# A fourth room for raw weights in the pairs stage, and the attention's mask table kept in DRAM

## The chip, the cores and the metric

The kernel runs on one NeuronCore of a Trainium2 chip. The metric is the device time of one execution in microseconds (us), as the median of several runs. A core has a matrix engine (TensorE, PE in the profile; its weight loads are PEld), three engines for elementwise work (VectorE or DVE, ScalarE or ACT, GpSimd or POOL) and a queue engine (SyncE, SP). Each engine runs its own instructions strictly in the order that was fixed at compile time and waits on semaphores for the others. Transfers (DMAs) are issued from SP, ACT and POOL and run on 16 DMA engines that all of them share.

## What is computed

One layer of a hybrid encoder for 1024 tokens and 1024 channels: a pooling mixer and a stick-breaking attention side by side, merged by gates, then a squared-ReLU MLP.

```
h    = rmsnorm(x, g_pre_mix)
proj = h @ w_in                        # u_pool | q | k | v, 512 columns each
y_pool = multiscale_pool(u_pool) @ w_br_pool
# attention, 8 heads of 64, blocks of 128 queries, mask: s < t
z    = (q @ k.T) * 64 ** -0.5
log_1mb = where(mask, log_sigmoid(-z), 0)
tail = cumsum(log_1mb, reverse) - log_1mb
attn = where(mask, exp(log_sigmoid(z) + tail), 0)
y_sb = (attn @ v) @ w_br_sb
gates = sigmoid(h @ w_gate + b_gate)   # 2048 columns
m    = (gates[:, :1024] * y_pool + gates[:, 1024:] * y_sb) @ w_out
x    = x + rmsnorm(m, g_post_mix)
h2   = rmsnorm(x, g_pre_mlp)
x    = x + rmsnorm(square(relu(h2 @ w_up)) @ w_down, g_post_mlp)
```

## The kernel before

All products are made in three matmuls of 128 x 128 x 512 (`mm3`, lines 110 to 112): every float32 operand is split into a rounded high part and the rest as a low part, and high x high, high x low and low x high are summed in a PSUM bank. The split of a raw weight tile of 128 x 1024 is a cast on ScalarE (high part) and a subtraction on VectorE (low part): `split_weights` (lines 1193 and 1194), or `prep` (lines 76 and 78) for the ordinary products.

The stages follow each other: `phase_in` (load x, first projections, the mask table, the operands of the pairs), `phase_project` (the pairs stage), `phase_attention` (attention with the branch products between), `phase_post`, `phase_mlp`.

**The pairs stage.** The gates (16 column groups) and the queries and keys (4 groups each) are made two groups at a time by a scheme that saves one product in eight: 7 half products of 12 matmuls for a pair instead of 8. `PAIRS` lists the 12 pairs: five of gates, then q, k, q, k, then three of gates. A pair needs two raw weight tiles r1 and r2 of 512 KB. `sw_weights(i)` is a generator that loads both and makes from them four split weights, a step at a time: `a1` from r1; `a22` from half of r2, then an add in place (line 519); three more adds in place (lines 521 to 523); `sb` from the changed r1; `sa` from the changed r2. The splits `a1` and `sa` lie in a ring of three rooms (`whi`, `wlo`) of the pool `weights`. `a22` and `sb` have rooms of their own for even pairs (`a0`, `s0` in the pool `tops`) and for odd ones (`a1`, `s1` in the pool `sw`).

The raw tiles have three rooms: two with the tag `wraw` in the pool `weights` and one, `wrawx`, in the pool `sw`. `self.raws = itertools.cycle(range(3))` deals them out in turn: pair 1 has `wrawx` and a `wraw`, pair 2 a `wraw` and `wrawx`, pair 3 two `wraw`, and so on; pair 0, which is loaded before the pool `sw` exists, has two `wraw`.

In `phase_project` the loop over the pairs makes the products of pair i, and at each product it takes one step of `sw_weights(i + 1)`, whose first step issues the loads of pair i + 1 on SP. A load waits until the room's last reader is done. The products of pair i are, in this order: `a1` x b11 and `a1` x b21 (`begin`), `sb` x t2, `sa` x t3, `sa` x t1, `a22` x t4, `sb` x b22. The operands b11 to t4 were made in `phase_in`; t2, t3 and t4 lie in the pool `tops`. The results go from PSUM through VectorE (lines 684, 695 to 705) to `result`: gates through a sigmoid into DRAM (`gscr`), queries and keys split (lines 542 and 543) into two staging rooms and from there into DRAM (`qscr`). Beside the products runs `later`: the pooling mixer (lines 560 to 610, operand `pq` on line 595, stored to `yscr`) and, after it, the values' pairs (`vpair`, `vs`).

**What fixes the order.** The code is traced in program order, and a scheduler at compile time orders each engine's instructions by when its model takes them to be ready. `issue_after(ins)` keeps an instruction behind another one on the same queue. The engine then keeps to that order, whatever is late.

**Where tiles lie.** Pools are stacked in the scratchpad, and the tiles of a pool lie in the order of their first allocation, from its lowest address up. The pool `sw` is opened when the pool `in_a`, with the tiles of x, is closed, and takes its place; the pools of the attention (`gt`, `att` and others) take the place of `tops` and `sw`. Pools opened with `reuse_waits="tile"` wait tile by tile: a new tile's first write waits for the last reader of the old tiles on that place, and no other. Both pools share one end, which is where `tops` ends. In the pool `in_a` the tile of `xs[0][0]` and `xs[0][1]` lies lowest, then the one of `xs[0][2]` and `xs[0][3]` and so on; `x00` in the code is `xs[0][0:4]`. In `tops` t2, t4 and t3 are followed by `a0` and `s0`; the gates' four rooms `gt` and the two rooms `oT` of the pool `gt` cover `a0` and `s0`.

**The mask table.** `phase_in` makes on GpSimd a table of 128 x 1024 bytes (line 303, 0 or 1 for "not in the past") into `self.past`, which has a fixed place in the pool `const`. Its only reader is the scan of the attention, `tensor_tensor_scan` on VectorE (line 801), one for each head and block of 128 queries, 64 in all.

**The start of the attention.** At the end of `phase_project` SP loads the queries and keys of the first two heads (lines 771 and 772), the pooling mixer's result y (line 730), the first gates (line 891, `gt`) and the values (line 755, `v`). Then the branch products (`job_pool`) run between the first heads' scores: each has 12 matmuls into one of two PSUM banks `dbr`, which VectorE empties into the gate tile (line 907), and the score products go through a sigmoid on ScalarE (line 799) and the scan on VectorE.

Of the kernel before, what the change touches and what calls it, by code (L numbers as in the profile page):

```python
# [19 lines left out]
F32 = mybir.dt.float32  # L20
# [12 lines left out]
P = 128  # L33
# [7 lines left out]
O_QK = O_U + N_U  # L41
O_V = O_QK + N_QK
O_G = O_V + N_V
# [9 lines left out]
class Block:  # L53
# [113 lines left out]
    def build(self):  # L167
        tc, nc = self.tc, self.nc
# [11 lines left out]
        cp = tc.alloc_tile_pool(name="const", bufs=1, side="left")  # L180
        self.wp = tc.alloc_tile_pool(name="weights", bufs=1, side="left")
        self.big = tc.alloc_tile_pool(name="big", bufs=1, side="left")
        dp = tc.alloc_tile_pool(name="scratch", bufs=1, space=DRAM)
# [4 lines left out]
        self.tscr = [dp.tile([P, 4, H], F32, name=f"tscr{f}") for f in range(4)]  # L188
        self.wscr = [[dp.tile([P, 4, 512], F32, name=f"wscr{n}_{q}") for q in range(4)] for n in range(2)]
        self.wsums = self.weight_sums()  # L190
        self.uscr = [dp.tile([P, 1024], F32, name=f"uscr{i}") for i in range(4)]
        self.qscr = [[dp.tile([192 - 64 * i, 1024], F32, name=f"qscr{i}_{j}") for j in range(8)] for i in range(2)]
        self.vscr = dp.tile([1 + P * NK, H], F32, name="vscr")
# [12 lines left out]
        self.gn = cp.tile([P, 32], F32, name="gn")  # L206
        self.eye = cp.tile([P, P], F32, name="eye")

        self.past = cp.tile([P, 1024], mybir.dt.uint8, name="past")
        self.rcnt = cp.tile([P, 16], F32, name="rcnt")  # L210

        self.rp = tc.alloc_tile_pool(name="row", bufs=1, side="left")
# [22 lines left out]
    def phase_in(self):  # L235
        tc, nc = self.tc, self.nc
# [5 lines left out]
        pa = tc.alloc_tile_pool(name="in_a", bufs=1, side="right")  # L242
# [11 lines left out]
        for g in range(3):  # L254
            if g < 2:
                raw = self.wp.tile([P, 1024], F32, name="wraw", tag="wraw", bufs=2)
            else:
                raw = early["t2_hi"][:, 0:2, :].rearrange("p k n -> p (k n)")
# [38 lines left out]
        past = early["t2_hi"][:, 2:4, :].rearrange("p k n -> p (k n)")  # L297
# [2 lines left out]
            out=past, in_=past, pattern=[[1, 1024]], compare_op=ALU.is_ge, fill=0.0, base=P - 1024,  # L300
            channel_multiplier=-1,
        )
        nc.gpsimd.tensor_copy(self.past, past)

        zero = early["t2_lo"][:, 1, :].bitcast(BF16)[:, :H]
        nc.vector.memset(zero, 0.0)
# [7 lines left out]
        for h in range(2):  # L314
# [3 lines left out]
            for k in range(NK):  # L318
                g = self.gn[:, k : k + 1]
# [136 lines left out]
        banks = [self.dps.tile([P, H], F32, name="dv", tag="d") for _ in range(2)]  # L456
        banks += [self.zps.tile([P, H], F32, name="dv", tag=t, bufs=n) for t, n in (("at", 3), ("z", 2))]
        gen = v_steps(1, (1, 2, 3, 0), banks)
        self.raws = itertools.cycle(range(3))
        first = self.sw_weights(0)  # L460
        for m in range(4):
            next(gen)
# [4 lines left out]
            k = m  # L467
# [28 lines left out]

    PAIRS = [("g", i) for i in range(5)] + [("q", 0), ("k", 0), ("q", 1), ("k", 1)] + [("g", i) for i in range(5, 8)]

    def sw_weights(self, i):

        nc = self.nc
        kind, f = self.PAIRS[i]
        a, n = (O_G + f, 8) if kind == "g" else (O_QK + 2 * f + (kind == "k"), 4)
        raw = []
        for g in (a, a + n):
            if next(self.raws) < 2 or self.sw_pools[1] is None:
                t = self.wp.tile([P, 1024], F32, name="wraw", tag="wraw", bufs=2)
            else:
                t = self.sw_pools[1].tile([P, 1024], F32, name="wrawx", tag="wrawx")
            nc.sync.dma_start(t, self.w[g])  # L510
            raw.append(t)
        r1, r2 = raw
        a11, a12, a21, a22 = r1[:, :512], r1[:, 512:], r2[:, :512], r2[:, 512:]
        w = self.sw[i] = {}
        w["a1"] = self.split_weights(r1, self.wp, "w", 3)
        yield
        pool = self.sw_pools[i % 2]
        w["a22"] = self.split_weights(a22, pool, f"a{i % 2}", 1, 512)
        nc.vector.tensor_add(a22, a21, a22)
        yield  # L520
        nc.vector.tensor_add(a21, a11, a21)
        nc.vector.tensor_add(a11, a11, a22)
        nc.vector.tensor_add(a12, a12, a11)
        yield
        w["sb"] = self.split_weights(r1, pool, f"s{i % 2}", 1)
        yield
        w["sa"] = self.split_weights(r2, self.wp, "w", 3)
# [118 lines left out]
    def phase_project(self):  # L646
        tc, nc = self.tc, self.nc
        pw = tc.alloc_tile_pool(name="sw", bufs=1, side="right", reuse_waits="tile")
        self.sw_pools[1] = pw

        def part(name):
            return pw.tile([P, H], F32, name=name, tag=name, bufs=1 + (name == "u"))
# [35 lines left out]
        for i, (kind, f1) in enumerate(self.PAIRS):  # L688
            f2 = f1 + (8 if kind == "g" else 2)
            w = self.sw[i]  # L690
            nxt = self.sw_weights(i + 1) if i + 1 < len(self.PAIRS) else iter(())
            if i not in begun:
                begin(i)
            u, v, c22 = begun[i], part("v"), part("c22")
            nc.vector.tensor_add(u, u, product(w["sb"], 0, "t2"))
            nc.vector.tensor_add(v, u, product(w["sa"], 0, "t3"))
            d = product(w["sa"], 512, "t1")
            nc.vector.tensor_add(c22, v, d)
            nc.vector.tensor_add(u, u, d)
            self.result(kind, f2, 1, c22, -1.0)  # L700
            if i == len(self.PAIRS) - 2:
                begin(i + 1)
            nc.vector.tensor_add(v, v, product(w["a22"], 0, "t4"))
            self.result(kind, f2, 0, v, -1.0)
            nc.vector.tensor_add(u, u, product(w["sb"], 512, "b22"))
            self.result(kind, f1, 1, u, 1.0)
# [9 lines left out]
            tc.alloc_tile_pool(name=n, bufs=1, side="right", reuse_waits="tile")  # L716
            for n in ("gt", "att", "qk", "oo", "att_s")
        )
        jobs = [("p", e + d, h) for e in range(0, 8, 2) for h in range(2) for d in range(2)]
        jobs += [("m", e, 0) for e in range(8)]  # L720
        self.fetch_order, self.fetches = jobs, {}
# [937 lines left out]
```

## Time and profile before

| | |
|---|---|
| three runs | 1271.15, 1271.83, 1272.05 us; median 1271.83 |
| the profiled execution | 1273.34 us, its span 1271.3 us |
| granted TensorE clock, mean | 0.999 |
| PE busy | 1241.4 us, 98% of the span, 5707 matmuls |
| weight loads (PEld) | 1020.3 us, 80% |
| VectorE | 967.8 us, 76% |
| ScalarE | 631.0 us, 50% |
| GpSimd | 179.7 us, 14% |
| DMA | 283.00 MB, mean 223 GB/s |
| pairs stage, first to last matmul | 97.2 to 347.7 us |
| loads into `wraw` on line 510 | 16, of 512 KB |
| loads into `wrawx` on line 510 | 8, of 512 KB; 3.5 to 9.0 us from issue to landing, median 8.7 |

The span runs from the first to the last instruction; the profiled execution is a little longer than its span, and both are compared like with like. A row of a timeline gives the start (us from the span's start), the duration, the engine, the line of the kernel, the operation, the tile written and those read, and in brackets the idle time of the engine before it and what ended that. "SPq" is the queue of SyncE, where the duration is that of the issue and not of the transfer. A row of the waits gives who waited for whom, the total in us, the number of waits and the longest.

### The profile page before, as it was taken

To read this page: it belongs to the slowest core of one execution; us is meant where nothing else is said; L and a number is where in the kernel's file an instruction comes from. 1 tells how busy PE (TensorE), PEld (TensorE's weight loads), DVE (VectorE), ACT (ScalarE), POOL (GpSimd) and SP (SyncE) were. 2 spreads that over 40 slices of the span, in tenths; PEclk is the share of its full clock that TensorE was granted. 3 is DMA by queue.
4 is the path that set the end of the run, shared out by engine and by line. 5 is a ranking of instruction groups with operands and counts; after the bars stand their busy time and mean duration, and the time that the engine had idled before them with its cause. 6 is when DMAs were issued, how large, how long until landed. Compare 5 with 4: busy or idle time off the path is not lost.

```text
span 1271.3 us, 16191 instructions
## 1 busy us (share of the span) xinstructions
PE 1241.4 (98%) x5707; PEld 1020.3 (80%) x5707; DVE 967.8 (76%) x1311; ACT 631.0 (50%) x1010; POOL 179.7 (14%) x319
## 2 busy tenths in 40 slices
PE   9999999998999999999999999999999999999998
PEld 6887778877877888787778878888888888888887
DVE  8849687766578898877797879887865565776975
ACT  8147334333456666674556546455454443344452
POOL 1212112342101111101100002222121110001000
PEclk9999999999999999999999999999999999999999
DMA  6586878977899674457648677676559996556552
GB/s 218 172 226 165 249 189 252 314 240 247 294 359 345 203 213 118 117 129 219 215 135 263 198 248 257 226 241 221 180 182 335 306 300 229 197 198 248 191 198 67
DMA packets 110305, 283.00 MB, mean 223 GB/s; under 512 B 12464, under 2 KB 17584, under 8 KB 109072
## 3 DMA queue, kind: packets, MB, share of 16 engines
q1 hardware_dynamic: 65696, 165.28, 37.9%
q0 software_dynamic: 30992, 91.13, 25.1%
q10 hardware_dynamic: 13536, 25.57, 6.2%
q8 instruction: 45, 0.74, 0.2%
q14 instruction: 36, 0.29, 0.1%
HBM read 208.52 MB, written 94.37 MB: 238 GB/s over the span
## 4 chain that ended last, share of the span: by engine, by line
PE 69%; DVE 13%; DMA 10%; issue 5%; ACT 3%; POOL 0%; ACTq 0%; SPq 0%; DVEq 0%; POOLq 0%
PE d L110 15%; PE d L111 15%; PE d L112 15%; PE sw L110 3%; PE sw L111 3%; PE sw L112 3%; PE o L838 2%; DVE T L801 2%; PE dbr L111 2%; PE dbr L112 2%; PE dbr L108 2%; DVE wlo L78 1%; DMA yscr<-win 1%; DMA wraw<-w 1%; PE at L814 1%
## 5 line engine op out<-in xcount | busy, mean ns | idle before, releaser
L111 PE MATMUL d<-blo,whi 128*128 128x512 f32 (+1 forms) x456 | 172.3, 378 | 0.0
L112 PE MATMUL d<-bhi,wlo 128*128 128x512 f32 (+1 forms) x456 | 171.9, 378 | 0.0
L110 PE MATMUL d<-bhi,whi 128*128 128x512 f32 (+1 forms) x456 | 168.7, 378 | 0.0
L112 PEld LDWEIGHTS d<-bhi,wlo 128*128 128x128 f32 x456 | 85.8, 188 | 16.1
L111 PEld LDWEIGHTS d<-blo,whi 128*128 128x128 f32 x456 | 85.7, 188 | 15.8
L110 PEld LDWEIGHTS d<-bhi,whi 128*128 128x128 f32 x456 | 85.5, 188 | 16.0
L801 DVE TENSOR_TENSOR_SCAN T<-T,past 128x512 f32<-128x512 f32 (+3 forms) x64 | 84.8, 1345 | 8.7 <-ACT T L799 8.4
L111 PE MATMUL d<-b_lo,whi 128*128 128x512 f32 x196 | 76.2, 390 | 1.2 <-DVE b_lo L1085 1.2
L110 PE MATMUL d<-b_hi,whi 128*128 128x512 f32 x196 | 75.7, 390 | 0.1
L112 PE MATMUL d<-b_hi,wlo 128*128 128x512 f32 x196 | 74.2, 389 | 0.0
L78 DVE TENSOR_TENSOR wlo<-wraw,whi 128x1024 fp32r<-128x1024 f32 x45 | 54.9, 1220 | 15.2 <-ACT whi L76 13.5
L76 ACT CAST whi<-wraw 128x1024 fp32r<-128x1024 f32 x45 | 47.5, 1056 | 37.9 <-DMA wraw<-w 19.0
L1382 DVE TENSOR_TENSOR wlo<-slots_hi,whi 128x1024 fp32r<-128x1024 f32 x29 | 35.5, 1223 | 37.3 <-ACT whi L1380 37.3
L1380 ACT CAST whi<-slots_hi 128x1024 fp32r<-128x1024 f32 x29 | 30.5, 1051 | 67.2 <-PE d L111 61.0
L799 ACT ACTIVATE T<-z 128x256 f32<-128x256 f32 (+2 forms) x96 | 44.8, 492 | 38.1 <-PE z L797 34.9
L1380 ACT CAST whi<-slots_lo 128x1024 fp32r<-128x1024 f32 x27 | 28.4, 1054 | 60.6 <-PE d L111 50.3
L110 PE MATMUL sw<-h_hi,whi 128*128 128x512 f32 x144 | 56.5, 392 | 1.9 <-DVE c L684 1.3
L111 PE MATMUL sw<-h_lo,whi 128*128 128x512 f32 x144 | 56.1, 389 | 0.0
L112 PE MATMUL sw<-h_hi,wlo 128*128 128x512 f32 x144 | 55.5, 390 | 0.1
L824 ACT CAST ahi<-at 128x512 fp32r<-128x512 f32 (+1 forms) x96 | 44.1, 484 | 22.8 <-PE at L814 19.8
L825 DVE TENSOR_TENSOR alo<-at,ahi 128x512 fp32r<-128x512 f32 (+1 forms) x96 | 50.0, 542 | 6.7 <-ACT ahi L824 6.6
L1193 ACT CAST whi<-wraw 128x1024 fp32r<-128x1024 f32 (+1 forms) x29 | 26.7, 928 | 54.7 <-PE d L111 24.2
(447 smaller groups left out, 3451.6 us busy)
## 6 DMA issues: line engine op xcount, KB each, us to landing
wraw<-w SPq DMA_DIRECT2D x57, 512.0 KB, 5.0
ext_b<-ascr SPq DMA_DIRECT2D x40, 512.0 KB, 7.0
wscr<-w POOLq DMA_DIRECT2D x32, 512.0 KB, 9.6
slots_hi<-w SPq DMA_DIRECT2D x10, 1024.0 KB, 8.0
slots_lo<-w SPq DMA_DIRECT2D x10, 1024.0 KB, 8.6
qq<-qscr SPq DMA_DIRECT2D x32, 256.0 KB, 5.1
pscr<-p SPq DMA_DIRECT2D x32, 256.0 KB, 3.9
u<-pscr ACTq DMA_DIRECT2D x32, 256.0 KB, 4.3
```

Of the source, the lines that this page charges most:

```text
L76: nc.scalar.copy(hi, raw)
L78: self.lows.append(nc.vector.tensor_sub(lo, raw, hi.bitcast(F32)).ins)
L110: nc.tensor.matmul(ps, wh, rh, start=first and i == 0, stop=False)
L111: nc.tensor.matmul(ps, wh, rl, start=False, stop=False)
L112: self.last_mm = nc.tensor.matmul(ps, wl, rh, start=False, stop=last and i == n - 1).ins
L799: self.after = nc.scalar.activation(f, z[:, :n], AF.Sigmoid, scale=-1.0)
L801: nc.vector.tensor_tensor_scan(f[:, ::-1], f[:, ::-1], past[:, ::-1], 1.0, ALU.mult, ALU.max)
L824: self.att_hi = nc.scalar.copy(hi[:, c:], at[:, c:]).ins
L825: self.att_lo = nc.vector.tensor_sub(lo[:, c:], at[:, c:], hi[:, c:].bitcast(F32)).ins
L1193: self.last_hi = nc.scalar.copy(hi, src).ins
L1380: last_split[0] = nc.scalar.copy(hi, src).ins
L1382: last_split[1] = nc.vector.tensor_sub(lo, src, hi.bitcast(F32)).ins
```

## The change

The raw tiles get four rooms: even pairs have both in `wraw`, odd pairs both in `wrawx`, which now has two rooms. The loads move out of `sw_weights` into `sw_raw(i)`. Pair 0 is loaded where it was. Pair 1 is loaded as soon as the pool `sw` is open, so that the two `wrawx` rooms are the first and lowest tiles of that pool. Every later pair i + 2 is loaded at the head of the loop for pair i: its rooms are those of pair i, whose last step was taken during pair i - 1. Before, the loads of pair i + 1 were issued in pair i.

The second `wrawx` room takes 4 KB in each partition of a scratchpad that is full. The mask table's 1 KB in `const` is given up for it: the table is made in the pool `in_a`, stored to DRAM (`mscr`) from GpSimd's queue, and loaded again on SP when the attention's pools are opened, into the lowest place of the pool `gt` (the pool grows downwards by 1 KB, over the last KB of t3's low half; the rooms `gt` and `oT` keep their places). The load is queued behind the first head's keys.

```diff
+        self.mscr = dp.tile([P, 1024], mybir.dt.uint8, name="mscr")
...
-        self.past = cp.tile([P, 1024], mybir.dt.uint8, name="past")
...
-        nc.gpsimd.tensor_copy(self.past, past)
+        table = pa.tile([P, 1024], mybir.dt.uint8, name="table")
+        nc.gpsimd.tensor_copy(table, past)
+        nc.gpsimd.dma_start(self.mscr, table)
...
-        self.raws = itertools.cycle(range(3))
+        self.raw = {}
...
-    def sw_weights(self, i):
-
-        nc = self.nc
+    def sw_raw(self, i):
+
         kind, f = self.PAIRS[i]
         a, n = (O_G + f, 8) if kind == "g" else (O_QK + 2 * f + (kind == "k"), 4)
-        raw = []
+        self.raw[i] = []
         for g in (a, a + n):
-            if next(self.raws) < 2 or self.sw_pools[1] is None:
+            if i % 2 == 0:
                 t = self.wp.tile([P, 1024], F32, name="wraw", tag="wraw", bufs=2)
             else:
-                t = self.sw_pools[1].tile([P, 1024], F32, name="wrawx", tag="wrawx")
-            nc.sync.dma_start(t, self.w[g])
-            raw.append(t)
-        r1, r2 = raw
+                t = self.sw_pools[1].tile([P, 1024], F32, name="wrawx", tag="wrawx", bufs=2)
+            self.nc.sync.dma_start(t, self.w[g])
+            self.raw[i].append(t)
+
+    def sw_weights(self, i):
+
+        nc = self.nc
+        kind, f = self.PAIRS[i]
+        if i == 0:
+            self.sw_raw(0)
+        r1, r2 = self.raw[i]
...
         self.sw_pools[1] = pw
+        self.sw_raw(1)
...
             w = self.sw[i]
+            if i + 2 < len(self.PAIRS):
+                self.sw_raw(i + 2)
             nxt = self.sw_weights(i + 1) if i + 1 < len(self.PAIRS) else iter(())
...
+        self.past = self.gp.tile([P, 1024], mybir.dt.uint8, name="past")
+        with tc.issue_after(self.head_load):
+            nc.sync.dma_start(self.past, self.mscr)
```

More of the change, by code (lines that the diff above doesn't have):

```diff
@@ L497 @@
     PAIRS = [("g", i) for i in range(5)] + [("q", 0), ("k", 0), ("q", 1), ("k", 1)] + [("g", i) for i in range(5, 8)]
+    def sw_raw(self, i):
+        kind, f = self.PAIRS[i]
+        a, n = (O_G + f, 8) if kind == "g" else (O_QK + 2 * f + (kind == "k"), 4)
+        self.raw[i] = []
+        for g in (a, a + n):
+            if i % 2 == 0:
+                t = self.wp.tile([P, 1024], F32, name="wraw", tag="wraw", bufs=2)
+            else:
+                t = self.sw_pools[1].tile([P, 1024], F32, name="wrawx", tag="wrawx", bufs=2)
+            self.nc.sync.dma_start(t, self.w[g])
+            self.raw[i].append(t)
     def sw_weights(self, i):
@@ L502, in sw_weights @@
         kind, f = self.PAIRS[i]
-        a, n = (O_G + f, 8) if kind == "g" else (O_QK + 2 * f + (kind == "k"), 4)
-        raw = []
-        for g in (a, a + n):
-            if next(self.raws) < 2 or self.sw_pools[1] is None:
-                t = self.wp.tile([P, 1024], F32, name="wraw", tag="wraw", bufs=2)
-            else:
-                t = self.sw_pools[1].tile([P, 1024], F32, name="wrawx", tag="wrawx")
-            nc.sync.dma_start(t, self.w[g])
-            raw.append(t)
-        r1, r2 = raw
+        if i == 0:
+            self.sw_raw(0)
+        r1, r2 = self.raw[i]
         a11, a12, a21, a22 = r1[:, :512], r1[:, 512:], r2[:, :512], r2[:, 512:]
```

## The prediction

> **What bounds the kernel now.** I read the page first, then the busy time by stage, then what the matrix engine waited for in the stage that the change touches, and last the order of time around each of those waits.
>
> ```profile
> span 1271.3 us, 16191 instructions
> ...
> PE 1241.4 (98%) x5707; PEld 1020.3 (80%) x5707; DVE 967.8 (76%) x1311; ACT 631.0 (50%) x1010; POOL 179.7 (14%) x319
> ```
>
> The matrix engine (PE) is busy for 98% of the span, so an edit that adds or removes none of its matmuls can win only what PE stands idle, 1271.3 - 1241.4 = 29.9 us in all. The profiled execution took 1273.34 us, 2.0 us more than its span, and the median of the three runs is 1271.83, 1.5 us below it. I sum against the span and take the result off the median, because stalls are absolute times.
>
> ```profile
> 97.00:350.00 253.00, 242.76 (x1046) 195.64 (x1045) 189.44 (x276) 105.70 (x146) 60.66 (x96) 0.99 0.80 246
> 350.00:400.00 50.00, 46.78 (x256) 38.95 (x255) 40.44 (x65) 31.35 (x80) 4.96 (x17) 1.00 0.97 349
> ```
>
> The columns are the stretch, its length, the busy time (and instructions) of PE, its weight loads, VectorE (DVE), ScalarE (ACT) and GpSimd (POOL), the granted clock, the share of the DMA engines and their GB/s. The first row is the pairs stage, 97 to 350 us: PE is idle for 10.2 us of it. The second is the start of the attention, where the transfers fill 97% of the DMA engines. These two rows are the field: the change can win at most some 10 us in the first (a little more with the clock, below), and it puts one more transfer into the second. What PE waited for in the first:
>
> ```profile
> PE sw L110 <- DVE u L705: 3.3, 1, 3.3
> PE sw L110 <- ACT whi L1193: 2.6, 2, 1.5
> PE sw L110 <- DVE c L684: 1.3, 1, 1.3
> PE sw L110 <- DVE u L695: 0.8, 2, 0.4
> PE dm L111 <- DVE pq L595: 0.7, 1, 0.7
> PE sw L112 <- DVE wlo L1194: 0.7, 2, 0.5
> ```
>
> Columns: total us, times, longest. Only the second and the last row are waits for split weights (L1193, L1194). The others are waits for a PSUM bank that DVE had not yet emptied, or for the pooling's operand (L595).
>
> **Part 1: the fourth room and the early load.** Follow one late weight, the second raw tile of pair 2, through the queues.
>
> ```profile
> 127.86 1.22 DVE L1194 TENSOR_TENSOR s1lo<-wrawx,s1hi 128x1024 fp32r<-128x1024 f32 x1
> 129.12 0.33 SPq L510 DMA_DIRECT2D wrawx<-w  x1
> 137.26 1.23 DVE L581 TENSOR_TENSOR win<-u 128x1023 f32<-128x1023 f32 x1 [6.86 <-DMA yscr<-win]
> 138.06 0.62 ACT L1193 CAST a0hi<-wrawx 128x512 fp32r<-128x512 f32 x1 [9.32 <-DMA wrawx<-w]
> 145.85 0.39 PE L112 MATMUL sw<-ph,wm 128*128 128x512 f32 x1
> 146.65 1.04 ACT L1193 CAST whi<-wrawx 128x1024 fp32r<-128x1024 f32 x1 [0.48 <-DVE wrawx L521]
> 147.75 0.50 PE L110 MATMUL sw<-ht_hi,whi 128*128 128x512 f32 x1 [1.51 <-ACT whi L1193]
> ```
>
> The room comes free at 129.08, when the previous pair's last reader ends. The load goes out at 129.12 and lands 8.9 us later. DVE then stands idle for 6.86 us up to 137.26 (another transfer's doing), and after that it must do both the pooling and this tile's adds, so the split that PE needs comes at 146.65. With four rooms this tile goes into a room that pair 0 left long before; its adds fit into the idle 6.86 us, and the wait at 147.75 goes. PE lost 147.75 - 145.85 = 1.90 from start to start where 0.23 is usual, so 1.67, and some 0.1 more at the next matmul: about 1.2 times the wait shown. The next pair repeats it (the third row below is pair 0, at the very start):
>
> ```profile
> 161.81 0.62 ACT L1193 CAST a1hi<-wraw 128x512 fp32r<-128x512 f32 x1 [8.74 <-DMA wraw<-w]
> 171.62 0.50 PE L110 MATMUL sw<-ht_hi,whi 128*128 128x512 f32 x1 [1.08 <-ACT whi L1193]
> 104.23 0.50 PE L112 MATMUL sw<-ht_hi,wlo 128*128 128x512 f32 x1 [0.50 <-DVE wlo L1194]
> ```
>
> Direct gain: 2.6 us of L1193, and 0.2 of the 0.7 us of L1194, because the 0.5 us at 104.23 belong to pair 0, whose loads do not move: 2.8 x 1.2 = 3.4 us.
>
> Indirect gain: L684, L695 and L595 are late because DVE runs strictly in order and the same late adds (L519 to L523, 0.69 us each) stand ahead of them. Together 0.8 + 0.7 + 1.3 = 2.8 us, 3.4 with the factor. Its bounds are 0 (the adds only move, and other work stands there instead) and 3.4. I take the middle, 1.7, since DVE is busy for 75% of this stage and has the room, but waits for the pooling's and the values' transfers that the change leaves alone.
>
> The largest wait I leave in place:
>
> ```profile
> 298.70 0.39 PE L112 MATMUL sw<-h_hi,wlo 128*128 128x512 f32 x1
> 300.46 0.69 DVE L543 SCALAR_TENSOR_TENSOR ks<-v,ks 128x512 fp32r<-128x512 f32 x1 [3.87 <-ACT ks L542]
> 302.41 0.77 PE L110 MATMUL sw<-ht_hi,a1hi 128*128 128x512 f32 x1 [3.32 <-DVE u L705]
> 305.93 0.40 PE L112 MATMUL sw<-ht_hi,a1lo 128*128 128x512 f32 x1
> ```
>
> DVE stood 3.87 us for the staged keys, whose two rooms wait for their stores; no raw weight is in that chain. It costs 3.71 - 0.23 = 3.5 us, and then eight matmuls take 305.93 - 302.41 = 3.52 instead of 1.84, another 1.7: after the gap PE ran at half speed for a while. The Trainium skill, in "TensorE: Matmul & The Clock Gate" (HAM oscillation), says that an idle gap over about 3.4 us halves the clock; this gap of 3.71 us agrees. Gain 0; upper bound 5.2, if a new order of DVE takes L705 ahead of the keys.
>
> Pair 1 pays for the new layout. Both its raw tiles now lie lowest in the pool, over x tiles of the first phase, and the second covers the one holding x00[2] and x00[3], which the t2 fill still reads.
>
> ```profile
> 104.21 0.33 SPq L510 DMA_DIRECT2D wraw<-w  x1
> 110.11 0.69 DVE L1085 TENSOR_TENSOR ht_lo<-x,ht_hi 128x512 fp32r<-128x512 f32 x1
> 116.66 0.69 DVE L519 TENSOR_TENSOR wraw<-wraw 128x512 f32<-128x512 f32 x1
> 123.80 2.36 DVE L1194 TENSOR_TENSOR wlo<-wraw,whi 128x1024 fp32r<-128x1024 f32 x2
> ```
>
> So that load goes out at 110.8 instead of 104.2. Queued behind it on SP (in order) are only the later raw loads, which are early now. With the 8.9 us of above it lands at 119.7, 3.0 us after DVE wanted it at 116.66, and if all of that reached the split, done at 126.2, PE could lose up to 3 us. With a landing of under 5.8 us it is not late at all. What covers it is that PE is still on pair 0 and that DVE has the pooling's work to put ahead; I take 0 and keep the 3 for the range.
>
> **Part 2: the mask table through DRAM.** Its store at the start is one more issue on POOL (14% busy) behind a 1.4 us cast with nothing of the attention waiting: 0. The load is what counts. It needs 1 KB in each partition that lies over the end of t3's low half, so it waits for the last pair's t3 product; it is on SP, in order; and the first scan (L801) now waits for it.
>
> ```profile
> 339.30 0.39 PE L112 MATMUL sw<-ht_hi,wlo 128*128 128x512 f32 x1
> 344.17 0.47 SPq L730 DMA_DIRECT2D ylo<-yscr  x1
> 345.17 5.69 SPq L891 DMA_DIRECT2D gt<-gscr  x4
> 352.40 2.18 SPq L755 DMA_DIRECT2D v<-sscr  x4
> 353.50 0.69 DVE L907 TENSOR_TENSOR gt<-gt,dbr 128x512 f32<-128x512 f32 x1 [4.92 <-DMA gt<-gscr]
> 354.10 2.07 DVE L801 TENSOR_TENSOR_SCAN T<-T,past 128x512 f32<-128x512 f32 x2
> 354.24 0.50 PE L110 MATMUL dbr<-yhi,whi 128*128 128x512 f32 x1
> 356.08 0.66 DVE L907 TENSOR_TENSOR gt<-gt,dbr 128x512 f32<-128x512 f32 x1
> ```
>
> The gates' rooms (gt) lie over tiles that pair 10 was the last to read, so they are free before 339.5 and the order most likely is gates, table, values (v): the table goes out at about 352.4, in the place of the first value load. Its transfer, 128 KB in rows of 1 KB, is in no row of before. The nearest rows are these (size, median to landing):
>
> ```profile
> gt<-gscr SPq DMA_DIRECT2D x20, 256.0 KB, 5.1
> qscr<-qs POOLq DMA_DIRECT2D x16, 128.0 KB, 4.7
> v<-sscr SPq DMA_DIRECT2D x8, 512.0 KB, 6.9
> ```
>
> I take 4.0 us, a little under the row of its size (an estimate): landed at 356.4, so the scans move from 354.1 to 356.4, 2.3 us. Behind them on DVE is L907 at 356.08, which empties the bank of the second branch product and ends at 356.74, then 359.0. PE has two banks for these products. It began the third at 354.24, needs 12 x 0.23 = 2.7 us for it, and wants the second's bank at about 357.0, or 357.4 with the score matmuls between: 1.6 us lost. The later loads move back by 128 KB at 349 GB/s, 0.4 us. Cost 2.0 us. Lower bound: issued at 340 ahead of the gates, it lands by 347 even at the 6.9 us of the value loads, and costs only the 0.4. The upper bound is the third rival's. By the Trainium skill, "DMA: Bandwidth & Descriptors" (Anatomy of one DMA), a transfer costs some 2.0 us plus its bytes over 436 GB/s, an estimate of 2.3 us here, by which the scans would be 0.6 us late and the total some 1.6 us better; the 4.7 us of this trace's 128 KB row speak against it.
>
> The rest is free: the attention's first weight tiles find their rooms empty sooner (pair 11 no longer uses them), but PE waits for none of them there.
>
> **Sum.** -3.4 - 1.7 + 2.0 = -3.1 us: 1271.83 - 3.1 = 1268.7 us (a profiled execution of about 1270.2, span 1268.2). About 0.2%, 2.5 us, is what a measurement of this kernel can tell from no change.
>
> **Rivals.**
> - *More goes than I count.* With the adds early, DVE's order changes in the query and key pairs too, and the wait for L705 goes with the clock's 1.7 us: -3.1 - 5.2 = -8.3, 1263.5; with half of it, 1266.1. For it: DVE's adds stand in that queue too. Against: its chain is the staging rooms. Chance 0.17.
> - *The gain is eaten in the stage.* PE then waits for the next late thing: the pooling's transfers hold DVE for 6.86 us whatever the weights do. Only the direct 3.4 us go, new waits of 1 us come, and the table takes 2.0: -0.4, 1271.4. For it: L705 and L684 are late without weights. Chance 0.18.
> - *Slower: the table is late.* If it is queued among the value loads or lands like them (6.9 us in the median row), the scans start at 359.3 or later, 5 us behind, and PE, with two banks and in order, stands 4.5 us; a gap above the 3.7 us seen at 302.41 also brings the half clock, 1.7 us. Cost 6.2 + 0.4 against 5.1 won: +1.5, 1273.3; with the indirect gain absent, +3.2, 1275.0. It decides from a landing at about 358.5. For it: 97% DMA share there. Against: the table is small and was ready to go at 339.5. Chance 0.20.
> - That the change doesn't do what it says has little room: each load's room and place are in its lines.
>
> My forecast has the remaining 0.45, with its own range of 1266.7 to 1271.0.
>
> **The numbers.** Two thirds of the forecast's chance lies below -2.5 us (0.30), and all of the first rival: faster 0.47. Same: a third of the forecast (0.15), the second rival (0.18), and a quarter of the third (0.05): 0.38. Slower: the rest of the third, 0.15. The range 1264.5 to 1273.6 leaves out the first rival's better half and the third's worse half, some 0.2.
>
> **What would show it.** Right: no wait of ACT on wraw or wrawx over 2 us between pairs 2 and 5; the waits for whi L1193 gone; PE idle in the pairs stage about 5 us less; the first scan 1 to 3 us later behind its gate product, waiting for the table's load; L705's wait still there. Wrong: PE idle in the pairs stage unchanged though the loads are early (the second rival), or a gap of over 3.5 us at the first scans with a granted clock below 1 there (the third).

## The result and the profile after

Beside the kernel before on the same chip the changed kernel took 1262.09 us (four runs, 1259.63 to 1264.59) against 1271.94 us (four runs, 1271.15 to 1274.60): a ratio of 0.9925, 95% interval 0.9906 to 0.9943, or 9.9 us. The forecast was 3.1 us, and its range ended at 1264.5 us. The profiled execution took 1264.59 us, with a span of 1262.8 us, 8.5 us under that of before.

The page of the changed kernel, then its pairs stage and the start of the attention by stretch (columns as before):

```profile
span 1262.8 us, 16190 instructions
...
PE 1239.2 (98%) x5707; PEld 1021.2 (81%) x5707; DVE 968.6 (77%) x1311; ACT 630.7 (50%) x1010; POOL 180.4 (14%) x320
```

```profile
97.00:350.00 253.00, 248.51 (x1082) 202.80 (x1081) 193.67 (x282) 107.59 (x151) 60.68 (x96) 0.99 0.83 257
350.00:400.00 50.00, 47.67 (x264) 39.74 (x263) 42.91 (x73) 34.04 (x88) 6.91 (x24) 1.00 0.99 360
```

PE has 1082 matmuls in the first stretch where it had 1046, and is idle for 4.5 us there instead of 10.2. What it still waited for (the last row is already the attention):

```profile
PE sw L112 <- DVE wlo L1208: 2.7, 2, 2.2
PE sw L110 <- ACT vs L633: 0.9, 1, 0.9
PE z L808 <- ACT T L813: 0.8, 1, 0.8
```

The waits for `whi`, for `pq` and for every sum are gone, L705's among them. One wait is new, and large. To see where the time went I count the stage's `sw` products by pair: 84 matmuls for each pair (those of the pooling left out), the start of every 84th taken from the trace. Two stretches are enough. A is pairs 1 to 5, mostly gates, with all of the pooling's matmuls between them; B is pairs 6 to 11, most of the queries and keys and the last gates, to the last matmul of the stage. A pair that nothing holds up takes 19.0 us, and one with a group of the pooling beside it 20.4.

| | A, pairs 1 to 5 | B, pairs 6 to 11 |
|---|---|---|
| undisturbed | 4 x 20.4 + 19.0 = 100.6 us | 6 x 19.0 = 114.0 us |
| before | 225.5 - 117.9 = 107.6 us | 347.5 - 225.5 = 122.0 us |
| changed | 222.8 - 117.9 = 104.9 us | 338.4 - 222.8 = 115.6 us |

So A, where the forecast had put nearly all of its gain, gave 2.7 us, and B, where it had put some 0.8 us (its share of L684), 6.4 us. That makes 9.1 us of a span that is 8.5 us shorter; the rest of the span differs little. By pair: in A pairs 2 to 5 gained 6.6 us (86.8 to 80.2) and pair 1 lost 3.9; in B pair 8 gained 2.2 (the wait for L684), pair 9, with the wait for pair 8's sum L705 and the half clock behind it, 5.8, and pair 10 lost 1.4.

The new wait is in pair 1. PE first, then VectorE (DVE) ahead of it:

```profile
125.50 0.40 PE L111 MATMUL sw<-h_lo,whi 128*128 128x512 f32 x1
128.10 0.50 PE L112 MATMUL sw<-ht_hi,wlo 128*128 128x512 f32 x1 [2.20 <-DVE wlo L1208]
128.44 0.52 PE L110 MATMUL sw<-ht_hi,whi 128*128 128x512 f32 x1
128.76 0.63 PE L111 MATMUL sw<-ht_lo,whi 128*128 128x512 f32 x1
```

```profile
120.82 0.69 DVE L1208 TENSOR_TENSOR a0lo<-wraw,a0hi 128x512 fp32r<-128x512 f32 x1
...
123.22 0.69 DVE L527 TENSOR_TENSOR wraw<-wraw 128x512 f32<-128x512 f32 x1
...
125.62 0.69 DVE L529 TENSOR_TENSOR wraw<-wraw 128x512 f32<-128x512 f32 x1
126.22 0.69 DVE L693 TENSOR_TENSOR c<-u,sw 128x512 f32<-128x512 f32 x1
126.82 1.22 DVE L1208 TENSOR_TENSOR wlo<-wrawx,whi 128x1024 fp32r<-128x1024 f32 x1
```

The split that PE needs (pair 1's `sa`) ends at 128.04. Ahead of it stand three instructions on `wraw`, which is pair 2's: some 0.6 us each, 1.8 us. They can stand there because pair 2's weights are early now. Nor is there a hole in which they would be free, for DVE is busy in all of these 28 us (the fifth number):

```profile
104.00:132.00 28.00, 25.54 (x101) 19.77 (x102) 28.00 (x43) 19.05 (x27) 9.47 (x13) 0.94 0.83 209
```

Behind the wait the matmuls last 0.63 instead of 0.39 us, and the granted clock of the stretch is 0.94: PE runs at half speed for some 3 us. Pair 1 takes 24.6 us, 4.2 more than undisturbed and 3.9 more than in before.

The mask table did not go where I had put it:

```profile
334.94 0.56 SPq L732 DMA_DIRECT2D past<-mscr  x1
339.32 2.87 SPq L905 DMA_DIRECT2D gt<-gscr  x3
...
346.12 0.98 ACT L813 ACTIVATE T<-z 128x512 f32<-128x512 f32 x2 [3.75 <-DMA gscr<-c]
...
346.75 2.08 DVE L815 TENSOR_TENSOR_SCAN T<-T,past 128x512 f32<-128x512 f32 x2 [1.81 <-ACT T L813]
...
DMA to landing us min/median/max: 8.6/8.6/8.6
```

It is issued ahead of the gates (L905), lands 8.6 us later at 343.5, and the first scan waits for ScalarE's sigmoid (ACT, L813), which itself stood behind a gate's store. The table holds nothing up.

### The profile page after: what moved, and what is told of

Its sections match the earlier page's. It is cut to its first block, busy times and chain, and to the rows that moved or that the text cites. A ratio compares the mean times of both kernels' runs of the same rounds, so it can differ in the third digit from the quotient of the medians.

```text
span 1262.8 us, 16190 instructions
## 1 busy us (share of the span) xinstructions
PE 1239.2 (98%) x5707; PEld 1021.2 (81%) x5707; DVE 968.6 (77%) x1311; ACT 630.7 (50%) x1010; POOL 180.4 (14%) x320
## 4 chain that ended last, share of the span: by engine, by line
PE 73%; DMA 9%; DVE 8%; issue 6%; ACT 2%; POOL 1%; SPq 0%; ACTq 0%; DVEq 0%; POOLq 0%
PE d L112 17%; PE d L111 17%; PE d L110 17%; DMA vpair<-vscr 3%; PE o L852 2%; PE dbr L108 2%; PE dbr L111 2%; PE dbr L112 2%; PE at L828 2%; DVE T L815 2%; DMA yscr<-win 1%; DMA qq<-qscr 1%; PE sw L112 1%; PE sw L111 1%; PE sw L110 1%
## 5 line engine op out<-in xcount | busy, mean ns | idle before, releaser
L813 ACT ACTIVATE T<-z 128x256 f32<-128x256 f32 (+2 forms) x96 | 45.2, 493 | 33.8 <-PE z L811 29.3
L838 ACT CAST ahi<-at 128x512 fp32r<-128x512 f32 (+1 forms) x96 | 44.1, 484 | 22.5 <-PE at L828 20.2
L1396 DVE TENSOR_TENSOR wlo<-slots_lo,whi 128x1024 fp32r<-128x1024 f32 x27 | 33.0, 1222 | 27.3 <-ACT whi L1394 27.0
```

Of the source, the lines that this page charges most:

```text
L813: self.after = nc.scalar.activation(f, z[:, :n], AF.Sigmoid, scale=-1.0)
L838: self.att_hi = nc.scalar.copy(hi[:, c:], at[:, c:]).ins
L1396: last_split[1] = nc.vector.tensor_sub(lo, src, hi.bitcast(F32)).ins
```

## The experiments

The theory after this profile: (1) in A the early weights remove the waits of pairs 2 and 3, but pair 2's adds, early too, push back pair 1's last split; (2) in B it isn't the lateness of the weights that went but an order on DVE. The scheduler made its order anew with the early weights in its model, and in pair 8 the sum that empties a PSUM bank now stands ahead of a split that waits for a staging room; (3) the table is free. The main rival to (2): the weights were late in B as well, and their adds held up the sums. In before, the order was ks<-v (L543, at 300.46), then an add, then L705. Now the sum is first:

```profile
290.04 0.68 DVE L716 TENSOR_TENSOR u<-u,sw 128x512 f32<-128x512 f32 x1
...
294.12 0.69 DVE L551 SCALAR_TENSOR_TENSOR ks<-v,ks 128x512 fp32r<-128x512 f32 x1 [1.30 <-ACT ks L550]
```

All twelve runs, in three groups; each group ran on one chip and has its own runs of the kernel before. A and B are of each one's profiled execution.

| kernel | median, us | before beside it, us | ratio (95%) | A, us | B, us |
|---|---|---|---|---|---|
| room_late | 1263.38 | 1269.96 | 0.9949 (0.9933 to 0.9966) | 106.6 | 115.1 |
| pair2_order | 1265.03 | 1269.96 | 0.9956 (0.9938 to 0.9973) | 105.3 | 119.0 |
| table_alone | 1268.84 | 1269.96 | 0.9990 (0.9978 to 1.0002) | 107.1 | 118.4 |
| late_all | 1264.99 | 1269.96 | 0.9969 (0.9956 to 0.9982) | 109.0 | 114.0 |
| before_order | 1269.21 | 1270.30 | 0.9987 (0.9972 to 1.0002) | 109.0 | 118.5 |
| order_back | 1265.39 | 1270.30 | 0.9964 (0.9949 to 0.9978) | 107.5 | 117.5 |
| late_gates | 1269.35 | 1270.30 | 0.9987 (0.9977 to 0.9998) | 112.4 | 114.0 |
| late_qk | 1265.20 | 1270.30 | 0.9954 (0.9938 to 0.9970) | 107.0 | 116.0 |
| changed_again | 1265.07 | 1269.99 | 0.9967 (0.9955 to 0.9979) | 106.5 | 115.8 |
| table_late | 1263.53 | 1269.99 | 0.9952 (0.9935 to 0.9968) | 107.7 | 115.0 |
| sums_first | 1258.65 | 1269.99 | 0.9913 (0.9899 to 0.9927) | 102.4 | 114.0 |
| before_sums | 1272.61 | 1269.99 | 1.0027 (1.0006 to 1.0048) | 111.0 | 117.4 |

**The changed kernel again.** 

> The changed kernel itself, unaltered, beside the other three. Theory: 6 to 10 us faster than the kernel before, as in its first two comparisons; in the profile the wait for wlo at 128 us, pair 2 to 8 without a wait over 1.5 us.

It came out 4.9 us faster by the medians, at the low end, with the wait at 128 us (2.38 us lost) and nothing over 1.5 us in pairs 2 to 8. Together with room_late (below), whose program has the same order on every engine, there are three measurements of the change: 9.9, 6.6 and 4.9 us. The sign is safe. The size varies with the chip and the executions, and the first one was the largest.

**room_late: does the earlier place in the code matter?**

```diff
-            if i + 2 < len(self.PAIRS):
-                self.sw_raw(i + 2)
...
-        if i == 0:
-            self.sw_raw(0)
+        if i != 1:
+            self.sw_raw(i)
```

> Four rooms, but the loads of pair i + 1 stand in the code where they stood before, at the first step of its weights, and not a pair sooner. Theory (the room does it: a load goes out when its room is free, wherever the code has it): the time of the changed kernel, 1262.1 us within 2.5, and all four raw loads of two pairs issued as in the changed kernel. Rival (the earlier place in the code does it): a part of the 9.8 us comes back, 1265 us or more.

1263.38 us, and in the pairs stage each engine's order of instructions is that of the changed kernel. SP issues nothing but these loads from the start of the stage until the first head's queries and keys at some 277 us, so a load goes out when its room is free. The room is the change; "a pair sooner" is only its name in the code.

**table_alone: the table without the room.** The table's part of the change's diff, put into the kernel before.

> The kernel before with the mask table through DRAM alone, three raw rooms as they were. Theory (the load is issued with the y loads, ahead of the gates, and is there before the first scan needs it): no difference, 1271.9 us within 1. Rival (my forecast's price, 2.0 us at the first scans, which the changed kernel hides behind some other gain): 1273.9 us.

1.1 us faster by the medians, an interval that holds no difference and leaves out the 2.0 us of cost. Its stage has before's order, and so it is a second profile of before's A and B: A 107.1, B 118.4 us. B is 3.6 us less than in the first profile, though the wait for the sum is there:

```profile
PE sw L110 <- ACT whi L1198: 2.6, 2, 1.5
PE sw L110 <- DVE u L707: 2.4, 1, 2.4
```

L707 is L705 of before. The 3.6 us lie in two places: pair 8 takes 19.0 us, without the wait for L684 (21.2 in before), and pair 9 takes 23.4 instead of 24.8. That B moves by this much between two executions of one order is the reason not to read the change's 6.4 us in B as its worth: against table_alone it is 2.5 to 3.4 us over the profiles with the changed order (115.0 to 115.8).

**table_late: nearer to the place that I had forecast.**

```diff
-        with tc.issue_after(self.head_load):
-            nc.sync.dma_start(self.past, self.mscr)
...
-                    self.load_values(0)
+                    with tc.issue_after(self.fetch_last):
+                        last = nc.sync.dma_start(self.past, self.mscr).ins
+                    with tc.issue_after(last):
+                        self.load_values(0)
```

> The changed kernel with the mask table's load queued behind the first gates and ahead of the values: the place that my forecast gave it. If the forecast's price for that place is right (landed at about 356 us, the first scans 2 us later, PE 1.6 + 0.4 us), it is 2 us slower than the changed kernel beside it. Rival (the first scan waits for ScalarE and the gates' adds anyway): within 0.7 us.

No slower than the changed kernel beside it (1263.53 against 1265.07 us).

```profile
342.65 0.38 SPq L749 DMA_DIRECT2D past<-mscr  x1
...
349.38 2.07 DVE L816 TENSOR_TENSOR_SCAN T<-T,past 128x512 f32<-128x512 f32 x2 [1.15 <-ACT T L814]
...
DMA to landing us min/median/max: 6.6/6.6/6.6
```

The table lands at 349.3 us, 0.1 us before the scan starts, and what the scan waits for last is still ScalarE. So the load is free here too, but with nothing to spare. It stands behind two of the four gates' loads and goes out 0.7 us after the start of the stage's last matmul, where my forecast had it behind all four, 4.9 us after that: what it would cost from there no run shows. What did fail is my 4.0 us for its landing. The Trainium skill's "DMA: Bandwidth & Descriptors" (Anatomy of one DMA) gives 2.0 us plus the bytes over 436 GB/s for transfers that GpSimd issues, an estimate of 2.3 us for 128 KB, which the prediction put on a load that SP issues; the two loads here, on SP and with the DMA engines busy all the time (the DMA share is 1.03 at 334 to 344 us and 1.06 at 340 to 350 us), took 8.6 and 6.6 us.

**late_all, late_gates, late_qk: the weights late again, the room kept.** In the pairs named, the second load waits for the split `sb` of the pair before it, as it did with three rooms.

```diff
+        if self.late(i):
+            info = mybir.DependencyInfo(mybir.DependencyClass.Sync, mybir.DependencyReason.DATA)
+            self.tc.add_manual_dep(ins, self.sb_split.name, info, reason="late")
+
+    def late(self, i):
+        return 2 <= i
```

with `2 <= i <= 5` and `6 <= i <= 9` for the other two.

> The changed kernel in which, from pair 2 on, the second raw load of every pair waits for the split sb of the pair before it, as it did with three rooms; the fourth room is there and stands empty in that time. Theory (all of the gain is the lateness of these loads, also where PE waited for a sum and not for a weight): the gain is given back, 1270 to 1273 us, and waits on L693 or L706 of the query and key pairs are back. Rival 1 (only the direct waits came from it, the query and key pairs' from another order): 1262.1 + 3.4 = 1265.5 us. Rival 2 (the gain is not the loads' at all): 1262 us.

> The changed kernel with late second raw loads in pairs 2 to 5 alone (each waits for the split sb of the pair before). My forecast's direct term: waits for split weights of pairs 2 and 3 come back, 3.4 us. But the order that the scheduler makes from it lets pair 8's L716 stand behind the split of its staged keys again, as in the kernel before. Theory (weights in pairs 2 and 3, order in pair 8): 3.4 us more in the first place, 2 to 5 us more in the second, 1.9 to 4.3 us less where the changed kernel stands at 128.34 us: 1264 to 1268 us, with a wait for L716 of pair 8. Rival (no order effect): 1265.5 us less the 128.34 us wait, 1262 to 1263 us, and no such wait.

> The changed kernel with late second raw loads in the query and key pairs 6 to 9 alone. In its order pair 8's L716 stands ahead of the split of ks<-v. Theory (order, not lateness): the time of the changed kernel, 1262 to 1263.5 us, the wait at 128.34 us still there, and no wait over 1.5 us in pairs 5 to 8. Rival (late weights hold VectorE in the query and key pairs): 3 to 6 us more, 1265 to 1268 us, with waits on L693, L706 or L716 there.

With all loads late, B is undisturbed (114.0 us), and most of the gain stays: 5.0 us by the medians, where room_late beside it has 6.6. My theory as I wrote it there (all of it comes from the loads) fell; rival 1 was right about B. Beside room_late the loss is 1.6 us and not its 3.4, since pair 1's wait goes as well (20.6 us against 23.0). The weights that VectorE splits and adds around the wait for pair 8's sum are pair 10's, and they were late in earnest: ScalarE's first cast of pair 10's second tile comes 14.0 us ahead of that pair's first product, against 14.4 in before and 18.8 in the changed kernel. In A, pairs 2 to 5 take 88.4 us against 83.6 in room_late, and the old wait is back:

```profile
PE sw L110 <- ACT whi L1214: 1.5, 1, 1.5
PE dm L111 <- DVE pq L610: 1.4, 1, 1.4
```

late_qk says less than it was meant to: with late weights in pairs 6 to 9 alone, B is 116.0 us against 115.0 to 115.8 without, no wait for a sum there is over 0.9 us, and its ratio is that of the changed kernel within the intervals. But it leaves pair 10's weights early (the same cast comes 18.1 us ahead), so that late weights cost PE little in B rests on late_all. Late_gates went worse than I expected, 1269.35 us: A takes 112.4 us, with a place that before did not have, pair 5 (22.5 us), which waits for its split `sb`:

```profile
PE sw L112 <- DVE s1lo L1215: 1.5, 1, 1.5
PE sw L110 <- ACT s1hi L1214: 1.3, 1, 1.3
```

And the wait for the sum in pair 8 that I expected from its order did not come (0.5 us in all), which I read so: a sum behind the split is costly only when the staging room is late as well.

**order_back and before_order: one rule of order each.** In pair 8, the sum behind the split of the staged keys in the changed kernel, and ahead of it in the kernel before. The scheduler moved a little more. In before_order one of pair 10's adds went ahead of the keys with the sum, and the other engines have the order of before. In order_back a split of pair 10 (`s0lo`) went ahead of the keys, and some instructions of VectorE and ScalarE behind this place changed theirs.

```diff
             self.result(kind, f2, 0, v, -1.0)
-            nc.vector.tensor_add(u, u, product(w["sb"], 512, "b22"))
+            with tc.issue_after(self.split) if i == 8 else contextlib.nullcontext():
+                nc.vector.tensor_add(u, u, product(w["sb"], 512, "b22"))
```

```diff
+            if i == 8:
+                add = nc.vector.tensor_add(u, u, product(w["sb"], 512, "b22")).ins
+                with tc.issue_after(add):
+                    self.result(kind, f2, 0, v, -1.0)
```

> The changed kernel with the order of the kernel before at that one place: in pair 8 the sum L716 stands behind the split of the staged keys (ks<-v). Theory (order alone costs there): in the changed kernel this split ends at 294.8 us, and PE wants the bank at 293.8 us, so a wait for L716 of some 1.0 to 2.0 us comes back and no half clock: 1 to 2 us slower than the changed kernel, 1264 us. Rival (the early weights took the wait away whatever the order): no wait for L716, the time of the changed kernel.

The wait comes back, in full view (L717 is the sum):

```profile
298.89 0.68 DVE L551 SCALAR_TENSOR_TENSOR ks<-v,ks 128x512 fp32r<-128x512 f32 x1
299.49 0.68 DVE L717 TENSOR_TENSOR u<-u,sw 128x512 f32<-128x512 f32 x1
```

```profile
300.23 0.50 PE L110 MATMUL sw<-ht_hi,a1hi 128*128 128x512 f32 x1 [3.18 <-DVE u L717]
300.56 0.39 PE L111 MATMUL sw<-ht_lo,a1hi 128*128 128x512 f32 x1
```

B rises to 117.5 us, about 2 above the changed kernel's, though every weight is early: the order alone makes this wait. It is longer than the 1.0 to 2.0 us expected, because the keys' split stands behind `s0lo`, which waits 1.1 us for ScalarE. The times cannot tell it: 1265.39 us is 2.0 over room_late and 0.3 over changed_again.

> The kernel before, in which one VectorE instruction of pair 8 changes place: the sum L705 that empties the PSUM bank for which PE waits at 302.41 us goes ahead of the split of the staged keys (ks<-v, L543) that waits for its room. Nothing of loads or rooms is touched, and every other engine keeps its order. Theory (what left the query and key pairs with the change is this order, which the scheduler chose anew, and not the lateness of the weights): the wait for L705 goes, 2.6 to 3.5 us, and the half clock behind it, 1.7 us: 4.3 to 5.2 us faster than the kernel before. Rival (the weights are late there, and PE then waits for the next of them): under 1.5 us, with a wait for another name between 300 and 307 us.

A miss in size: the time is the rival's. The wait is gone from that place (the sum is done at 298.55, PE has no gap there), but B is 118.5 us against 118.4 in table_alone, and the time is 1.1 us better by the medians with an interval that reaches 1. The time came back at other places:

```profile
PE sw L110 <- DVE u L695: 2.2, 3, 1.4
PE sw L110 <- ACT vs L625: 1.7, 1, 1.7
PE sw L110 <- DVE c L684: 0.8, 1, 0.8
```

```profile
320.30 0.69 DVE L622 TENSOR_TENSOR vpair<-vpair 128x512 f32<-128x512 f32 x1 [4.52 <-DMA vpair<-vscr]
```

In B it is the values: ScalarE's cast (L625) comes after this 4.5 us wait of DVE for a load, and PE behind it. So B of before holds several such places, and curing one lets the next show. The changed kernel's order happens to be free of nearly all of them.

**pair2_order: the new wait of pair 1.** Pair 2's first split and adds only behind pair 1's `sa`.

```diff
+        with self.tc.issue_after(self.first_sa) if i == 2 else contextlib.nullcontext():
+            w["a22"] = self.split_weights(a22, pool, f"a{i % 2}", 1, 512)
+            nc.vector.tensor_add(a22, a21, a22)
```

and the same for the next three adds.

> The changed kernel with one new rule of order: VectorE makes pair 2's first split and adds only behind pair 1's last split (sa). Theory (in the changed kernel three early instructions of pair 2, 1.8 us, stand on VectorE ahead of the split for which PE waits at 128.34 us; this costs 2.4 us, and 1.9 us more in matmuls at half speed behind it): both go, 4.3 us below the profiled 1264.6 us, so 1260.3 us. Rival (pair 1's own weights are late because its second load went out 6.6 us later, and the wait only changes its name): within 1 us of the changed kernel's 1264.6 in a profile, with a wait of 2 us or more still between 124 and 136 us.

The wait at 128 us is gone, and two others are there, so nothing is won (1265.03 against room_late's 1263.38 us):

```profile
PE sw L110 <- DVE c L697: 3.1, 1, 3.1
PE sw L110 <- DVE u L710: 2.5, 1, 2.5
```

```profile
138.18 1.23 DVE L593 TENSOR_TENSOR win<-u 128x1023 f32<-128x1023 f32 x1 [3.68 <-DMA yscr<-win]
...
143.99 0.68 DVE L710 TENSOR_TENSOR u<-u,sw 128x512 f32<-128x512 f32 x1
```

The second wait is pair 1's sum L710, which stands behind the pooling's window sum; that one waits 3.7 us for its room's store. In the changed kernel, as I read it, the stall at 128 us makes PE so late that this doesn't show. The first one is in the query and key pairs, where the new rule of order had the scheduler deal out everything anew.

**sums_first and before_sums: rules in place of luck.** The pooling's window sums, and the splits of staged queries and keys, each behind the latest sum that empties a bank:

```diff
+            for _ in range(g == 1):
+                yield
...
-                nc.vector.tensor_add(nxt[:, sh:], cur[:, sh:], cur[:, : 1024 - sh])
-                nc.vector.tensor_copy(nxt[:, :sh], cur[:, :sh])
+                with self.tc.issue_after(self.emptied) if g else contextlib.nullcontext():
+                    nc.vector.tensor_add(nxt[:, sh:], cur[:, sh:], cur[:, : 1024 - sh])
+                    nc.vector.tensor_copy(nxt[:, :sh], cur[:, :sh])
...
+            if kind != "g":
+                with tc.issue_after(self.emptied):
+                    self.result(kind, f2, 1, c22, -1.0)
```

`self.emptied` is set at each of these sums, and the split of v follows the last sum of its pair likewise. sums_first has this and pair2_order's rule on the changed kernel; before_sums has it on the kernel before, without the extra step for the second group.

> The changed kernel with rules of order for VectorE: pair 2's first split and adds behind pair 1's last split; the pooling's window sums (which wait for stores) behind the last traced sum that empties a PSUM bank, and one step later for the second group; the splits of staged queries and keys behind the next such sum. Theory (PE waits in this stage because sums that empty banks, or one split, stand on VectorE behind something that waits for a transfer): the 2.4 us at 128 us go, pairs 1 to 3 lose 3 us less, and no wait for L706-like sums appears in the query and key pairs: 3 to 5 us faster than the changed kernel beside it. Rival (VectorE is simply full between 104 and 132 us, and the waits only move): within 1.5 us of it.

> The kernel before, three raw rooms and the table in place, with the same two rules of order (window sums and staged splits behind the sums that empty PSUM banks). If order is the larger part of the change's gain: 3 to 6 us faster than the kernel before, with only the waits for whi of pairs 2 and 3 left. If the fourth room is: under 2 us.

sums_first took 1258.65 us (1258.41 to 1260.41), 11.3 us less than before and 6.4 less than the changed kernel beside it, more than the 3 to 5 expected: the best of all. B is undisturbed, A within 1.8 us of it, PE idle for 1.1 us of the stage, and one wait is left:

```profile
97.00:350.00 253.00, 251.91 (x1115) 206.96 (x1113) 200.51 (x290) 111.80 (x159) 60.44 (x96) 1.00 0.84 264
```

```profile
PE sw L110 <- DVE c L700: 1.1, 1, 1.1
```

The same rules with three rooms lost: 1272.61 us. The wait for the late weights grew to 4.6 us at one place, with the half clock behind it:

```profile
PE sw L110 <- ACT whi L1202: 4.8, 2, 4.6
PE dm L110 <- ACT ph L595: 1.7, 1, 1.7
```

So neither half gives the 11.3 us: the room without the rules 4.9 us here, the rules without the room a loss of 2.6. As I read it, the room makes the weights early enough for such an order, and the order decides whether that reaches PE; the two runs don't have quite the same rules.

## Why the prediction was wrong, point by point

- **L705's wait, "Gain 0; upper bound 5.2": the step that failed.** I reasoned that no raw weight is in its chain, which late_all bears out, and concluded that the change would leave it. But the order on DVE is no constant: the scheduler makes it from its model, in which the loads' times had changed. The prediction named this case ("if a new order of DVE takes L705 ahead of the keys") and gave it 0.17. It happened: no profile with the changed order has the wait, late_all is without it though its weights are late, and order_back shows that the order alone makes it. Pair 9 takes 19.0 us where the two profiles of before's order have 24.8 and 23.4; pair 10 gives 0.8 to 1.7 us of that back, in part waiting for the values' split, and B as a whole is 2.5 to 6.4 us shorter, by which profile of before one takes. The prediction also held the gap's 3.71 us, which are from start to start, against a rule on idle time; the idle time is the 3.32 us in the row's brackets.
- **Direct gain 3.4: the waits went, the size is about right.** No wait for `whi` is left. Pairs 2 to 5 take 80.2 to 83.9 us in the four profiles with the changed order, against 86.8 and 86.4 in the two of before's: 2.5 to 6.6 us for the direct and the indirect gain together, where the forecast's share in these pairs is about 4.3. Making the loads late again costs them 4.7 us (late_all against room_late). My sign for it (no wait of ScalarE for a raw tile over 2 us) was too strict. It still waited,

```profile
136.93 1.05 ACT L1207 CAST whi<-wrawx 128x1024 fp32r<-128x1024 f32 x1 [6.07 <-DMA wrawx<-w]
```

  but PE did not.
- **Indirect gain 1.7 of 3.4.** L695 and L595, both in A, and L684 in B are gone from the profile of the changed kernel. room_late and table_late have other waits for sums in A, of 0.4 to 1.0 us each. What the three are worth by themselves cannot be told apart from the direct gain.
- **Pair 1 at cost 0, bound 3: failed, by another way than the bound's.** The second load did go out at 110.85 us as worked out and landed 3.7 us later, within the 5.8 us that I had called in time. What was late was pair 1's last split, behind pair 2's adds; with these behind it (pair2_order), or late again (late_all, late_gates), the wait goes. The moved load had a part in it all the same: pair 1's first add ran at 120.22 us where before has it at 116.66, with none of pair 2's adds ahead of it yet. I had looked at whether the moved load is late, and not at what the other loads, now early, put ahead of the split on an engine without a hole. Pair 1 took 2.2 to 3.0 us more than in before, and 3.9 where the half clock followed.
- **Table, 2.0 us: failed in place, and its landing was mis-sized.** It is issued ahead of the gates, and it costs nothing measurable there or in table_late, since the first scan waits for ScalarE. My lower bound was the case that came. The landing takes 8.6 and 6.6 us where I had 4.0; the rival "the table is late" (0.20) was right about that and wrong about the place.
- **The sum.** -3.1 us became -9.9, -6.6 and -4.9. The first rival's mechanism came true, and its -8.3 us lies among these three. That its figure fits is partly luck: it holds the table's 2.0 us, which were not paid, and leaves out pair 1's 2.2 to 3.9, which were.

What stays open: why the wait for L684 came in one of two executions of before's order and not in the other (most of the 3.6 us by which B differs), and which of sums_first's three rules carries how much of its 6.4 us.

## What to carry to other kernels

A change to when data arrives is also a change to the order that a scheduler writes down, far from the place of the edit: look for the sums that empty PSUM banks, and at what stands ahead of each on its in-order queue, before and after. Work that is made early is not free if its engine is full in that stretch; it needs a rule that keeps it behind the older work. And when an edit gains more than its mechanism explains, put the order back by itself: here one rule of order brought a wait of 3.2 us back, and stated rules of order, on top of the room, were worth 6.4 us where the room by itself had given 4.9.

## What the hardware showed that I had not expected

Whether the clock halves after a wait is not settled by its length. The gap of 2.60 us at 128 us, from one matmul's start to the next, occurs in six profiles with the changed kernel's order in pair 1. In two (the changed kernel, changed_again) the next matmuls ran at half speed; in four (room_late, late_qk, order_back, table_late) they did not, as here in room_late:

```profile
128.86 0.50 PE L112 MATMUL sw<-ht_hi,wlo 128*128 128x512 f32 x1 [2.21 <-DVE wlo L1206]
129.20 0.40 PE L110 MATMUL sw<-ht_hi,whi 128*128 128x512 f32 x1
129.44 0.39 PE L111 MATMUL sw<-ht_lo,whi 128*128 128x512 f32 x1
```

order_back's gap of 3.56 us at 300 us was not followed by it either, while table_alone's of 2.82 us was. What decides is where a gap falls. In every trace, up to the kernel's end, a stretch at half speed lasts 3.41 us or a multiple of it, and from the first time that the clock is full to each later change there is a whole number of such windows (36 in the changed kernel, 87 in before). The window with the gap and the next one, in the changed kernel and then in room_late (the third number is PE's busy time, the third from the end the granted clock):

```profile
125.14:128.55 3.41, 1.21 (x5) 0.70 (x5) 3.41 (x5) 3.41 (x6) 0.66 (x2) 1.00 0.83 200
128.55:131.96 3.41, 3.41 (x10) 2.63 (x9) 3.41 (x5) 1.77 (x3) 0.55 (x1) 0.50 1.00 206
```

```profile
124.44:127.86 3.42, 2.22 (x10) 1.33 (x8) 3.42 (x7) 3.42 (x6) 0.96 (x1) 1.00 0.61 192
127.86:131.27 3.41, 2.41 (x11) 1.99 (x12) 3.41 (x5) 2.88 (x5) 0.58 (x1) 1.00 1.07 168
```

In the changed kernel one window holds most of the gap; in room_late two windows share it. From the pairs stage to the last 10 us of the kernel, the fourteen traces have eight windows in which PE was busy for less than 1.5 us; each was followed by one at half speed, and no window with more than 1.7 us was. order_back's 3.56 us are shared as well, with 1.82 and 1.83 us of work in the two windows.

The Trainium skill's "TensorE: Matmul & The Clock Gate" (HAM oscillation) puts the danger at idle gaps over about 3.4 us, and the prediction took that as a line; the idle gaps of 2.20 us in the changed kernel and 2.43 us in table_alone, both followed by half speed, disagree. The Trainium skill says on the same page (Part 1: The HAM clock gate) that the activity window, of about 3.4 us, runs freely and doesn't start with the work; the traces agree, with the 3.41 us above. A wait of some 2.6 us is thus to be priced with a chance of some 1.6 us on top (pair 1 takes 24.6 us in both profiles with it, and 23.0 in three of the four without).
